# Plain projection weights: the low part starts as the negative of the high part, and a DMA adds the weights to it

## The chip, the cores and the metric

The kernel runs on one core of a Trainium2 chip. The metric is the device time of one execution in microseconds. The core has five engines that run side by side and wait for each other through semaphores: TensorE (PE in the profile, its weight loads PEld), VectorE (DVE), ScalarE (ACT), GpSimd (POOL) and SyncE (SP). SP, ACT and POOL can issue transfers (DMAs); 16 DMA engines carry them out. Each engine works through its own instructions in the order of the program.

## The reference

One decoder layer for 512 tokens of width 1024. What matters here is its first product, the input projection, which gives queries, keys and values of three attention groups, the input of a state space model, and gate logits:

```python
proj = x @ w_in[layer]
q = proj[..., :QKV_WIDTH]...
k = proj[..., QKV_WIDTH:2 * QKV_WIDTH]...
v = proj[..., 2 * QKV_WIDTH:3 * QKV_WIDTH]...
u = proj[..., 3 * QKV_WIDTH:3 * QKV_WIDTH + SSM_WIDTH]
gate_logits = proj[..., 3 * QKV_WIDTH + SSM_WIDTH:]
q = apply_rope(q, pos)
k = apply_rope(k, pos)
```

Behind it come windowed attention, the state space model `s5_ssm`, a merge with gates, an output projection, layer norm, a feed-forward network and a second layer norm. All of it is float32.

## The kernel before

**Products in three parts.** PE multiplies in a rounded float type (`F32R`). To keep float32's precision each operand is held as two tiles: `hi`, the value rounded to that type, and `lo`, the value less `hi`. `mm3` (lines 208 to 211) makes one product out of three matmuls: hi by hi, hi by lo, lo by hi. So every weight needs its `lo` before PE can get past the first matmul of a step.

**How weights arrive.** The class `Weights` (line 100) keeps a list of units. A unit is 128 x 2048 float32 (1 MB) in DRAM. SP loads it whole into a `raw` tile (`load`, lines 115 to 124; two such tiles). `split` (line 140) then turns one half of it, 128 x 1024, into a pair `whi`, `wlo`: ACT copies the half into `whi` (line 202), DVE subtracts `whi` from the raw half into `wlo` (line 203). There are three slots for such pairs. A step of the kernel uses one pair; at its end `release` frees the slot and calls `split` for the pair three steps ahead, whose ACT copy waits until PE has finished the step. After the second half of a unit `split` issues the next load.

**The steps.** The list `STEPS` has 36 entries, numbered n, one per weight pair: u (0 to 3), v of the first group (4 to 7), gates (8 to 19), k (20 to 23), q (24 to 27), v of the other two groups (28 to 35). Splits have the same numbers. Steps 0 to 3 have their own code, so the first split through the class is number 4; splits 4 to 35 belong to units of `w_in`. A step is 24 matmuls of 512 columns. Gate, k and q steps are `gate_tile` and `qk_tile` around `proj_tile`; v steps are `v_tiles`. Later stages (five "quads" of the input projection, then the GLU, branch, output and feed-forward weights) use the same class with other units, or write their own pairs.

**What else stands on the engines.** The order is written out by hand: `run_fill(n)` puts other work between or into the steps, by a table of step numbers (`at_step`). DVE carries the state space model's small operations, handed out a few at a time (`late`). ACT also copies x into time order (`copy_time`, line 510), copies u out (599), and applies the gates' function (958). POOL has little but DMAs. In step order these are: three parked gate blocks of 1 MB (`park_gates`, line 946); the rope's half turns, four adding DMAs of 32 partitions each after steps 21, 23, 25 and 27 (`turn_half`, line 768, called by `qk_tile` as soon as DVE has written its two rope products `kq` and `zk` or `zq`); and two loads of x in another order, 1 MB each (`fetch_x`, line 1068, at 30.6), which wait until the state space model's output has left the tile they go to (`ydr`).

Of the kernel before, what the change touches and what calls it, by code (L numbers as in the profile page):

```python
# [10 lines left out]
F32 = mybir.dt.float32  # L11
# [3 lines left out]
ALU = mybir.AluOpType  # L15
# [84 lines left out]
class Weights:  # L100


    def __init__(self, nc, pool, split):
        self.nc, self.split_to = nc, split
        self.units, self.raw, self.views = [], {}, {}
        self.free = deque((pool, n) for n in range(3))
        self.held = deque()
        self.pool = pool
        self.n_dma = self.n_split = 0
        self.jobs, self.loads, self.after, self.extra = {}, {}, None, None  # L110
# [29 lines left out]
    def split(self):  # L140
        n = self.n_split
        if n == 2 * len(self.units):
            return
        if self.jobs.get(n):
            self.jobs[n].popleft()()
            return
        self.flush()
        self.n_split += 1
        m, u = divmod(n, 2)
        slot = self.units[m][2]  # L150
        if slot is None:
            hi, lo = self.take_slot(n)
        else:
            z = slot(f"w{n}", F32R)
            hi, lo = z[:, 0:1024], z[:, 1024:2048]
        self.split_to(hi, lo, self.raw[m][:, 1024 * u : 1024 * (u + 1)])
        self.put(n, hi, lo)
        if u == 1:
            del self.raw[m]
            self.load()  # L160
# [14 lines left out]
def emit(ctx, tc, i, out):  # L175
# [42 lines left out]
    def kslice(pair, k, cols=slice(None)):  # L218
        return pair[0][k // 4][:, k % 4, cols], pair[1][k // 4][:, k % 4, cols]
# [21 lines left out]
    def home(n, name, dt=F32):  # L241
        return gat(n[1:], name, dt) if isinstance(n, str) else big(n, name, dt)

    w = Weights(nc, wp, split)
    out_homes = deque(("g0", 2, 6, 3))
    w.add(None, 8)
    for n in range(2, N_GLU, 2):
# [5 lines left out]
        else:  # L253
            w.add(i["w_in"][2 + 6 * g + 2 * "kqv".index(kind) + un], 2 if kind == "v" else 8)
    quad_first = 2 * len(w.units)
    for un in range(2):
        w.add(i["w_glu"][un], 4)
    for un in range(4):
# [235 lines left out]
    for k in range(KT):  # L494
        (xh, uh), (xl, ul) = ((z[k // 4][:, k % 4, :] for z in (xp[n], wup[n])) for n in range(2))
        raw = raws[k // 2][:, k % 2]
        if k == 0:
            late.take(4)
            continue
        for n, (hi, lo) in enumerate(((xh, xl), (uh, ul))):  # L500
            split(hi, lo, raw[:, 2 * n : 2 * n + 2].rearrange("p e c -> p (e c)"))
        late.take(4 if k < 2 else 10)
# [761 lines left out]
    for n in range(8):  # L1264
        ws = w.views[N_BR + n]
        src = (gh_, gl_) if n < 4 else (merged["h"], merged["l"])
# [21 lines left out]
        if n >= 4:  # L1288
            for ch, t0, _ in ts_:
                hi, lo = kslice(mx, ch)  # L1290
# [442 lines left out]
def build(inputs):  # L1733
    import concourse.bacc as bacc

    a = {k: np.asarray(v) for k, v in inputs.items()}
    arrays = {f"in_{k}": np.ascontiguousarray(v) for k, v in {**layout(a), **constants()}.items()}
    nc = bacc.Bacc("TRN2", target_bir_lowering=False, num_devices=1)
    aps = {k[3:]: nc.dram_tensor(k, v.shape, mybir.dt.from_np(v.dtype), kind="ExternalInput").ap()
           for k, v in arrays.items()}  # L1740
    out = nc.dram_tensor("out_dram", (S, D), F32, kind="ExternalOutput").ap()
    with tile.TileContext(nc) as tc:
        with ExitStack() as ctx:
            with tc.manual_schedule():
                emit(ctx, tc, aps, out)
    return nc, arrays
# [8 lines left out]
```

## Time and profile before

| | |
|---|---|
| time, median of 2 runs | 834.8 us (834.32 to 835.27) |
| the profiled execution | 835.37 us, span 833.6 us |
| granted TensorE clock, mean | 0.997 |
| PE busy | 822.0 us (99%) |
| DVE / ACT / POOL busy | 621.1 / 381.9 / 70.2 us |
| moved by DMA | 109.08 MB |
| queue 1 (SP), queue 0 (POOL), share of 16 engines | 31.9%, 8.8% |

The span runs from the first to the last instruction of the profiled execution; its own time has some more around it. Busy is the time in which an engine had an instruction in work. The strips of digits cut the span into 40 slices of 20.8 us; a digit is the busy share in tenths. A row of a timeline gives start, duration, engine, line, operation, tiles and in brackets the idle time before it with what ended that. A row of a table of stages gives the stretch, its length, busy time and number of instructions of each engine, the clock, the busy share of the DMA engines and GB/s. A queue's row gives packets, MB and the time its packets took as a share of 16 engines over the window asked for.

### The profile page before, as it was taken

The page shows a single profiled execution, that of the slowest core. Times are in us where ns is not written, and L with a number is a line of the kernel's source. Part 1 is how long each engine was busy: PE and PEld are TensorE (multiplying, and loading weights), DVE is VectorE, ACT ScalarE, POOL GpSimd, SP SyncE. Part 2 cuts the span into 40 slices and gives each one's busy share as a digit, 9 for nine tenths or more (in the row PEclk, how much of TensorE's full clock was granted, in tenths as well). Part 3 has the DMA queues.
Part 4 walks back from the last instruction along what each step waited for, and adds up shares of the span by engine and source line. Part 5 has one row for each costly group of instructions (what it writes and reads, how often), then busy time and mean ns, then how long its engine had stood idle before and what let it go on. Part 6 is the DMA issues. An engine that isn't in the chain of part 4 may idle for free.

```text
span 833.6 us, 13772 instructions
## 1 busy us (share of the span) xinstructions
PE 822.0 (99%) x5656; PEld 736.3 (88%) x5656; DVE 621.1 (75%) x1013; ACT 381.9 (46%) x579; POOL 70.2 (8%) x84
## 2 busy tenths in 40 slices
PE   9999999999999999999999999999999999999996
PEld 7888888888899989988888899999999999888885
DVE  6976899673879799556796798888888887523347
ACT  6964332145557535774242354445545456322210
POOL 0000001310011333000000410000000000000005
PEclk9999999999999999999999999999999999999998
DMA  8733534746235655651624162333322212722103
GB/s 336 190 106 137 161 138 127 167 117 198 77 88 141 129 107 112 210 208 51 252 101 152 51 223 87 112 118 114 107 101 101 103 52 101 303 101 87 65 1 101
DMA packets 29598, 109.08 MB, mean 131 GB/s; under 512 B 7392, under 2 KB 12256, under 8 KB 19936
## 3 DMA queue, kind: packets, MB, share of 16 engines
q1 hardware_dynamic: 23664, 90.79, 31.9%
q0 software_dynamic: 4240, 15.73, 8.8%
q10 hardware_dynamic: 1632, 1.70, 0.6%
q8 instruction: 44, 0.72, 0.4%
q14 instruction: 18, 0.15, 0.1%
HBM read 92.21 MB, written 9.70 MB: 122 GB/s over the span
## 4 chain that ended last, share of the span: by engine, by line
PE 68%; DVE 4%; DMA 2%; ACT 1%; issue 1%; POOL 0%; DVEq 0%; ACTq 0%
PE qx L1151 5%; PE dn L209 5%; PE dn L210 5%; PE dn L211 5%; PE qz L1151 2%; PE qy L1151 2%; PE wo L209 2%; PE wo L210 2%; PE b L210 2%; PE wo L211 2%; PE b L209 2%; PE b L211 2%; PE o L864 2%; PE fs9x L1498 1%; PE fs8x L1498 1%; PE fs7x L1498 1%
## 5 line engine op out<-in xcount | busy, mean ns | idle before, releaser
L203 DVE TENSOR_TENSOR wlo<-raw,whi 128x1024 fp32r<-128x1024 f32 x74 | 90.8, 1230 | 93.3 <-ACT whi L202 93.3
L202 ACT CAST whi<-raw 128x1024 fp32r<-128x1024 f32 x74 | 77.3, 1049 | 105.3 <-PE dn L211 63.5
L1466 ACT CAST whi<-sums 128x1024 fp32r<-128x1024 f32 x40 | 42.0, 1049 | 95.6 <-DVE sums L345 95.6
L209 PE MATMUL dn<-whi,ffh 128*128 128x512 f32 x168 | 65.4, 389 | 0.0
L210 PE MATMUL dn<-wlo,ffh 128*128 128x512 f32 x168 | 65.4, 389 | 0.0
L211 PE MATMUL dn<-whi,ffl 128*128 128x512 f32 x168 | 65.4, 389 | 0.0
L345 DVE TENSOR_TENSOR wlo<-sums,whi 128x1024 fp32r<-128x1024 f32 x40 | 48.7, 1220 | 0.0
L1122 ACT CAST whi_q<-rq 128x1024 fp32r<-128x1024 f32 x28 | 29.2, 1052 | 41.8 <-DVE rq L345 41.8
L345 DVE TENSOR_TENSOR wlo_q<-rq,whi_q 128x1024 fp32r<-128x1024 f32 x28 | 34.1, 1222 | 12.9 <-ACT whi_q L1122 12.6
L209 PE MATMUL pg<-x_hi,whi 128*128 128x512 f32 x96 | 37.6, 392 | 0.0
L210 PE MATMUL pg<-x_lo,whi 128*128 128x512 f32 x96 | 37.4, 389 | 0.0
L211 PEld LDWEIGHTS dn<-whi,ffl 128*128 128x128 f32 x168 | 31.5, 188 | 6.6
L211 PE MATMUL pg<-x_hi,wlo 128*128 128x512 f32 x96 | 37.4, 389 | 0.0
L209 PEld LDWEIGHTS dn<-whi,ffh 128*128 128x128 f32 x168 | 31.5, 188 | 6.6
L210 PEld LDWEIGHTS dn<-wlo,ffh 128*128 128x128 f32 x168 | 31.5, 188 | 6.4
L843 ACT ACTIVATE un<-un,st 128x256 f32<-128x256 f32 (+1 forms) x64 | 30.8, 483 | 13.2 <-DVE st L841 13.2
L768 POOL DMA_DIRECT2D kq<-qz x32 | 25.2, 1313 | 108.7 <-PE s L830 48.2
L1309 POOL TENSOR_TENSOR mvb<-mvb,epsb 128x1 f32<-128x1 f32 x4 | 3.9, 987 | 329.2 <-DVE mvb L337 329.2
L958 ACT ACTIVATE gt<-pg,bgate 128x512 f32<-128x512 f32 x12 | 8.3, 690 | 42.9 <-PE pg L211 42.9
L345 DVE TENSOR_TENSOR wlo<-ra,whi 128x1024 fp32r<-128x1024 f32 x20 | 24.4, 1222 | 1.8 <-ACT whi L1466 1.8
L209 PE MATMUL pv<-whi,x_hi 128*128 128x512 f32 x64 | 25.4, 396 | 0.0
L210 PE MATMUL pv<-wlo,x_hi 128*128 128x512 f32 x64 | 25.0, 390 | 0.0
(731 smaller groups left out, 2733.3 us busy)
## 6 DMA issues: line engine op xcount, KB each, us to landing
raw<-in_w_in SPq DMA_DIRECT2D x16, 1024.0 KB, 4.8
raw<-in_w_dn SPq DMA_DIRECT2D x11, 1024.0 KB, 4.8
ra<-in_w_gu SPq DMA_DIRECT2D x10, 1024.0 KB, 4.8
rb<-in_w_gu SPq DMA_DIRECT2D x10, 1024.0 KB, 4.8
rq<-in_w_quad SPq DMA_DIRECT2D x16, 512.0 KB, 4.3
kq<-qz POOLq DMA_DIRECT2D x32, 128.0 KB, 5.2
raw<-in_w_br SPq DMA_DIRECT2D x4, 1024.0 KB, 4.8
raw<-in_w_out SPq DMA_DIRECT2D x4, 1024.0 KB, 4.8
```

The lines of the kernel that those rows point to most:

```text
L202: act.copy(hi, src)
L203: dve.tensor_tensor(lo, src, hi.bitcast(F32), op=ALU.subtract)
L209: pe.matmul(dst, a[0], b[0], start=first, stop=False)
L210: pe.matmul(dst, a[0], b[1], start=False, stop=False)
L211: pe.matmul(dst, a[1], b[0], start=False, stop=last)
L345: eng.tensor_tensor(o, a, b, op=op)
L768: pool.dma_start(dst[32 * q : 32 * q + 32], z[32 * (q ^ 1) : 32 * (q ^ 1) + 32], accum_op=ALU.add)
L843: act.activation(pt, pt, AF.Exp, bias=mneg, scale=-1.0, accum_out=zsum)
L1122: act.copy(hi, src)
L1151: pe.matmul(d[:, 256 * e : 256 * e + 256], p_[:, e, k, :], q_[:, k, :], start=(first and e == k == m == 0), stop=(k == 3 and m == 2), skip ...
L1466: act.copy(hi, src)
L1498: pe.matmul(c, p_[:, e, k, :], q_[:, k, :], start=(b is not None and e == k == m == 0), stop=(k == 3 and m == 2), skip_group_check=True)
```

## The change

For the units of `w_in` (the first 18 units; `n_early` holds that number) `split` no longer lets DVE subtract. ACT copies the raw half into `whi` as before, ACT then writes minus `whi` into `wlo`, and POOL issues a DMA that reads the same half of the weights from DRAM a second time and adds it to `wlo`. All other weights are split as before. Splits 4 to 35 go this way, 32 in all.

```diff
         else:
             z = slot(f"w{n}", F32R)
             hi, lo = z[:, 0:1024], z[:, 1024:2048]
-        self.split_to(hi, lo, self.raw[m][:, 1024 * u : 1024 * (u + 1)])
+        src = self.raw[m][:, 1024 * u : 1024 * (u + 1)]
+        if m < self.n_early:
+            self.nc.scalar.copy(hi, src)
+            self.nc.scalar.mul(lo, hi.bitcast(F32), -1.0)
+            self.nc.gpsimd.dma_start(lo, self.units[m][0][:, 1024 * u : 1024 * (u + 1)], accum_op=ALU.add)
+        else:
+            self.split_to(hi, lo, src)
         self.put(n, hi, lo)
         if u == 1:
             del self.raw[m]
@@
     quad_first = 2 * len(w.units)
+    w.n_early = len(w.units)
     for un in range(2):
         w.add(i["w_glu"][un], 4)
```

On POOL, from the first parked gate block to the loads of x, the order before (`gdr` is the DRAM copy of a gate block, `kq` the tile that a rope turn adds to, `zk` and `zq` the products that it turns, `xf` x in another order):

```order
L946 DMA gdr<-gt_710 128x2048
L946 DMA gdr<-gt_986 128x2048
L946 DMA gdr<-gt_1166 128x2048
L768 DMA kq_1353<-zk_1352 32x2x512 x4
L768 DMA kq_1428<-zk_1427 32x2x512 x4
L768 DMA kq_1353<-zq_1498 32x2x512 x4
L768 DMA kq_1428<-zq_1567 32x2x512 x4
L1068 DMA xf_1909<-in_xk 128x2048
L1068 DMA xf_1911<-in_xk 128x2048
```

And now, from the first rope turn on (`wlo_24` is the low part for step 24; the lines are seven further on in the changed file):

```order
L775 DMA kq_1372<-zk_1371 32x2x512 x4
L160 DMA wlo_24_1417<-in_w_in 128x1024
L160 DMA wlo_25_1453<-in_w_in 128x1024
L775 DMA kq_1449<-zk_1448 32x2x512 x4
L160 DMA wlo_26_1492<-in_w_in 128x1024
L160 DMA wlo_27_1525<-in_w_in 128x1024
L775 DMA kq_1372<-zq_1521 32x2x512 x4
L160 DMA wlo_28_1563<-in_w_in 128x1024
```

The weights' DMA for split 24, 26 and 28 stands right behind the four DMAs of a rope turn. Further on in the same engine's order now, at the loads of x:

```order
L160 DMA wlo_32_1842<-in_w_in 128x1024
L160 DMA wlo_33_1919<-in_w_in 128x1024
L1075 DMA xf_1939<-in_xk 128x2048
L1075 DMA xf_1941<-in_xk 128x2048
L160 DMA wlo_34_1958<-in_w_in 128x1024
L160 DMA wlo_35_2015<-in_w_in 128x1024
```

Before, nothing stood behind the two loads of x until the next rope turn; now splits 34 and 35 do.

On ACT, at the first splits, the order before (`xt` is x in time order, `usb` the copy of u, `raw_128` the first unit):

```order
L510 COPY xt_262<-x_lo_95 128x2x4x128
L202 CAST whi_4_265<-raw_128 128x1024
L202 CAST whi_5_281<-raw_128 128x1024
L510 COPY xt_299<-x_hi_93 128x2x4x128
L510 COPY xt_299<-x_lo_95 128x2x4x128
L599 COPY usb<-pu_315 128x512
```

and now:

```order
L517 COPY xt_262<-x_lo_95 128x2x4x128
L158 CAST whi_4_265<-raw_128 128x1024
L159 ACTIVATE wlo_4_266<-whi_4_265 128x1024
L158 CAST whi_5_282<-raw_128 128x1024
L159 ACTIVATE wlo_5_283<-whi_5_282 128x1024
L517 COPY xt_301<-x_hi_93 128x2x4x128
L517 COPY xt_301<-x_lo_95 128x2x4x128
L606 COPY usb<-pu_317 128x512
```

Each copy has a negation behind it, and the copies of x and of u come after both.

## The prediction

> **What bounds the kernel now.** I read the page's busy row and its 40 slices first, then the waits of the tensor engine, then a table by stage, then timelines at the places where the change acts.
>
> ```profile
> PE 822.0 (99%) x5656; PEld 736.3 (88%) x5656; DVE 621.1 (75%) x1013; ACT 381.9 (46%) x579; POOL 70.2 (8%) x84
> PE   9999999999999999999999999999999999999996
> DMA  8733534746235655651624162333322212722103
> PE warm_b L289 <- DVE warm L285: 1.1, 1, 1.1
> PE fs10x L1498 <- DVE quad L345: 0.8, 1, 0.8
> PE qx L1151 <- ACT qsnap L1184: 0.7, 1, 0.7
> PE kb L566 <- issue: 0.5, 1, 0.5
> PE s L830 <- DMA kq<-qz: 0.4, 1, 0.4
> ```
>
> PE works without a gap: its five waits come to 3.5 us. So nothing taken off DVE can make the kernel faster by more than these, and only 0.5 us of them lies in the part that the change touches. What matters is whether the new way of making the second operand makes PE wait. The table by stage covers that part: 27 us (step 4, first use of such an operand) to 206 us (the last split, number 35).
>
> ```profile
> 27.00:60.00 33.00, 33.00 (x256) 27.39 (x259) 29.98 (x107) 24.72 (x28) 0.00 (x0) 1.00 0.61 160
> 60.00:126.00 66.00, 65.54 (x426) 54.29 (x419) 52.51 (x116) 24.02 (x31) 1.82 (x3) 1.00 0.42 143
> 126.00:180.00 54.00, 54.00 (x392) 44.83 (x394) 41.96 (x45) 14.21 (x21) 13.76 (x16) 1.00 0.60 132
> 180.00:206.00 26.00, 26.00 (x151) 21.22 (x143) 11.59 (x30) 14.66 (x33) 1.17 (x2) 1.00 0.61 199
> ```
>
> The columns are the stretch, its length, then busy us of PE, PE's weight loads, DVE, ACT and POOL, the clock, the DMA share and GB/s. PE is full in all four; ACT is fairly full in the first (24.72 of 33); DMA is busy 0.61, 0.42, 0.60 and 0.61, which is 20.1 + 27.7 + 32.4 + 15.9 = 96 us of 179.
>
> **What goes, what comes.** 32 splits change (numbers 4 to 35).
>
> ```profile
> L203 DVE TENSOR_TENSOR wlo<-raw,whi 128x1024 fp32r<-128x1024 f32 x74 | 90.8, 1230 | 93.3 <-ACT whi L202 93.3
> L202 ACT CAST whi<-raw 128x1024 fp32r<-128x1024 f32 x74 | 77.3, 1049 | 105.3 <-PE dn L211 63.5
> ```
>
> DVE loses 32 x 1.23 = 39 us. PE waited for DVE nowhere in this part, so that is worth nothing by itself. ACT gets 32 negations; none stands in the trace, and I price one as the copy of the same shape, 1.05 us: 34 us. POOL gets 32 issues and the DMA engines 32 transfers of 0.5 MB that add into their destination.
>
> *Price of one such transfer.* The only adding ones in the trace are the rope turns (kq, line 768; four of 128 KB make 0.5 MB), the nearest plain ones on the same queue are xf. The two rows are queue 0 from 138 to 149 us and from 197 to 206 us; packets, MB, share of 16 engines.
>
> ```profile
> q0 software_dynamic: 320, 0.52, 39.5%
> ...
> q0 software_dynamic: 288, 2.10, 57.4%
> ```
>
> The turns take 0.395 x 11 = 4.3 us per 0.5 MB. Plain: 0.574 x 9 = 5.2 us for 2.1 MB, 1.3 us per 0.5 MB. Adding needs two streams read (source, destination) where a plain transfer reads one, so 2.6 us is the low end, 4.3 the high one. I take 2.6: a turn reads and writes 32 partitions with both ends on chip, the new transfer has 128 partitions and one end in DRAM, as xf has. By the first price the load is 96 + 32 x 2.6 = 179 us for 179 us, by the second 234.
>
> *Latency in the gate steps (8 to 19).* Rows of ACT's timeline (start, us):
>
> ```profile
> 85.08 0.69 ACT L958 ACTIVATE gt<-pg,bgate 128x512 f32<-128x512 f32 x1 [3.81 <-PE pg L211]
> 90.52 0.69 ACT L958 ACTIVATE gt<-pg,bgate 128x512 f32<-128x512 f32 x1 [3.81 <-PE pg L211]
> 91.11 1.04 ACT L202 CAST whi<-raw 128x1024 fp32r<-128x1024 f32 x1
> ```
>
> A step lasts 5.44 us. Its slot is refilled for the step three later, so the refill has two steps, 10.9 us. From the step's end at 90.5: copy done 92.2, negation 93.2. From issue to the first bytes I read the DMA strip of 138 to 149 us (40 slices of 0.275 us) against POOL's row:
>
> ```profile
> 138.48 3.49 POOL L768 DMA_DIRECT2D kq<-zk  x4 [13.81 <-DMA raw<-in_w_in]
> DMA  5000000999937999979998872000199327999999
> ```
>
> Bytes flow from the eighth slice, 139.9: 1.45 us after the issue; they end near 145. So here bytes flow at 94.7 and end at 97.3, with a 0.2 us landing at 97.5; or at 100.1 where the 1 MB load of the next raw weights takes turns with them (2.6 us more). Due at 101.4. Covered by 1.3 to 3.9 us. Only the three parked gate blocks (1 MB each, 2.6 us ahead in the same queue) can break this: 0 to 3 us, I take 1. The Trainium skill, DMA: Bandwidth & Descriptors (Anatomy of one DMA), gives 2.0 us plus bytes over 436 GB/s for a transfer from this queue, an estimate of 3.2 us for 0.5 MB where my rows give 1.45 + 2.6 + 0.2 = 4.25; by it each refill would come 1 us sooner and the sum below fall by about 4. It names no price for adding.
>
> *Start (step 4).*
>
> ```profile
> 22.11 2.03 ACT L202 CAST whi<-raw 128x1024 fp32r<-128x1024 f32 x2
> 27.51 0.39 PE L210 MATMUL pv<-wlo,xt 128*128 128x512 f32 x1
> ```
>
> Copy 23.1, negation 24.1, bytes from 25.6 to 28.2, landed 28.4; PE wants it at 27.5. 0.9 us late, 3.5 beside a raw load. I take 1.5.
>
> *ACT up to 60 us.* It has 24.72 of 33 us; two negations push into it and six lie in it: 24.7 + 8.4 = 33.1. ACT is then full, and the copies of x in time order, of u and of the state inputs come up to 6 us later. PE has some of these one to two steps ahead. 0 to 6, I take 3.5.
>
> *The four rope turns (after steps 21, 23, 25, 27).* The new issue stands on POOL behind the turn's four issues, and those wait for DVE. Rows of ACT and DVE:
>
> ```profile
> 133.81 1.06 ACT L202 CAST whi<-raw 128x1024 fp32r<-128x1024 f32 x1 [4.38 <-PE pk L210]
> 137.09 1.08 DVE L345 TENSOR_TENSOR zk<-pk,rope 128x512 f32<-128x512 f32 x1
> 144.69 1.06 ACT L202 CAST whi<-raw 128x1024 fp32r<-128x1024 f32 x1 [4.38 <-PE pk L210]
> ```
>
> Step 21 ends at 133.8; zk is there 4.4 us later, the turn's bytes end at about 144.9, 11.1 us after the step, and the bytes for split 24 follow in the same queue: 11.1 + 2.6 + 0.2 = 13.9 us, due after 10.9. DVE is behind here because of queued state work and three subtractions; without the subtractions zk could come after its two products, about 2.2 us from the step's end, and all this 2.2 us sooner: 11.7, late by 0.8. With a raw load beside it 2.6 more, 3.4; with DVE as late as now, 5.6. Four times 0.8 to 5.6 is 3 to 22; I take 2.75 each, 11: half with a raw load, little DVE delay.
>
> *After 180 us.* The two xf loads wait on POOL for ydr and stand ahead of split 34.
>
> ```profile
> 197.28 1.17 POOL L1068 DMA_DIRECT2D xf<-in_xk  x2 [24.88 <-DMA ydr<-ysb]
> 203.48 1.05 ACT L202 CAST whi<-raw 128x1024 fp32r<-128x1024 f32 x1 [1.99 <-PE pv L211]
> ```
>
> Their 5.2 us of bytes end about 204, split 34's at 206.8; step 32 ends at 203.4 and step 34 starts one step after, about 208.9. Covered by 2 us; 0 to 3, I take 2, for the load of 0.61 + 3 x 2.6 / 26 = 0.91.
>
> Sum: 1 + 1.5 + 3.5 + 11 + 2 = 19 us, between 5 and 37 with all the ends. The profiled execution took 835.37 us (span 833.6), 0.6 above the median of 834.8: 835.4 + 19 = 854.
>
> **The rivals.**
>
> *A, the queue is full.* If an adding transfer costs what the turns show, 4.3 us, the load by stage (7, 12, 10 and 3 of the splits start in the four stretches, the first at 22 us) is 20.1 + 7 x 4.3 = 50 for 33, 27.7 + 12 x 4.3 = 79 for 66, 32.4 + 10 x 4.3 = 75 for 54, 15.9 + 3 x 4.3 = 29 for 26: 17 + 13 + 21 + 3 = 54 us over, and PE waits for all of it: 889. For it: it is the only adding transfer measured. Against it: the shape of the turns. The point of change is (179 - 96) / 32 = 2.6 us per transfer, so my own price sits on the edge.
>
> *B, not slower.* DVE is the place: with 39 us taken off it, zk comes 2.2 us after the step, the raw loads, which no longer wait for DVE's subtraction, fall before the turns, and each turn's bytes end early enough. Then split 24 lands within 10.9 us and only the start is late: 835 + 1.5, some 837. It decides at 0.8 us per turn, less than my reading of when the bytes end is worth. Against it: the stage from 126 to 180 us would have 32.4 + 26 = 58 us of DMA for 54.
>
> *C, the clock.* At the end of the kernel PE stops, and the clock goes:
>
> ```profile
> 825.41 0.28 PE L211 MATMUL dq<-whi,ffl 128*128 128x192 f32 x1
> 829.00:833.00 4.00, 0.00 (x0) 0.00 (x0) 0.61 (x1) 0.00 (x0) 0.00 (x0) 0.50 0.36 135
> ```
>
> It is halved about 3.3 us after the last matmul (the 0.50 begins a little before 829). Waits of that length in four to eight places would each be followed by work at half rate; if the clock comes back as slowly as it goes, 3.3 us at half rate lose 1.7 us each, 7 to 13 us more than the forecast, around 864. The Trainium skill, TensorE: Matmul & The Clock Gate (Part 1), says that an idle window of about 3.4 us halves the clock and that as much sustained work restores it; the end of this trace agrees with the first half, no row here shows the second.
>
> *D, faster.* A gain above 2% has no place: PE's waits are 3.5 us in all.
>
> **How the numbers follow.** Forecast 0.56, A 0.20, B 0.14, C 0.08, D or anything faster 0.02. The time is the forecast's, 854. Two per cent, about what a measurement of this kernel tells from no change, is 16.7 us, so the line is 851.5. The forecast's own range, 840 to 872, lies about two thirds above it: 0.38 slower, 0.18 within; with A and C slower is 0.66, with B same is 0.32. The range for 8 in 10 leaves most of B out below and the end of A above: 842 to 895.
>
> **What would show it.** Right: PE waits on `wlo` after steps 21 to 27 of 1 to 5 us each, waits at step 4 of 1 to 3 us, none above 1 us in the gate steps but after a parked block; ACT near 1.0 busy up to 60 us; queue 0 with about 2.6 us of engine time per new transfer; the clock at 1.00 throughout. Wrong: engine time near 4 us and PE waiting in every step from 8 on (A), no waits but the first (B), a clock under 1 between 27 and 240 us (C), or a negation or an issue on POOL that costs far more than the 1.05 and 0.9 us read here.

## The result, and the profile after

| | before | after |
|---|---|---|
| time, median | 834.8 us | 873.4 us (873.18 to 873.66) |
| ratio | | 1.0463, 95% between 1.0418 and 1.0508 |
| profiled execution, span | 833.6 us | 871.0 us |
| granted clock, mean | 0.997 | 0.981 |
| queue 0 (POOL's), MB and share of 16 engines | 15.73, 8.8% | 32.51, 18.9% |

The change costs 38.6 us. All times here are medians of fast executions; one execution of the kernel with 32 small DMAs took 1162.7 us at a granted clock of 0.654 and is not among them. The page of the kernel after, with the rows that answer to those of before: busy times, and the slices of PE, the clock and DMA.

```profile
PE 832.3 (96%) x5656; PEld 742.7 (85%) x5656; DVE 585.5 (67%) x981; ACT 416.0 (48%) x611; POOL 98.4 (11%) x116
PE   9799999779899999999999999999999999999995
PEclk9899999889989999999999999999999999999998
DMA  9986999894922655564254216223322322622103
```

DVE has lost 35.6 us of work and ACT has gained 34.1, nearly as the edit says, and neither matters. What matters is that PE, once at 9 in every slice but the last, shows three 7 and an 8 among its first eleven, that the clock's row shows an 8 in four places ahead of the last slice, and that DMA is at 8 or 9 in slices where it was at 3 to 7. The waits of PE in the kernel after (us in all, times, longest):

```profile
PE pv L216 <- DMA wlo<-in_w_in: 18.1, 3, 6.3
PE pq L217 <- DMA wlo<-in_w_in: 6.0, 1, 6.0
```

Four waits for the new transfer come to 24.1 us; nothing else on the list is above the 1.1 us that was the largest before. They lie at step 4, at splits 24 and 28, and at split 34. Each is followed by a stretch at half the clock. The chain that ended last, in order of time, shows the first (start, length, what):

```profile
24.15 9.38 DMA wlo<-in_w_in
...
33.57 0.80 PE pv L216
34.36 0.43 PE pv L217
...
39.41 0.24 PE pv L217
```

The transfer is issued at 24.15 and lands 9.4 us later. PE then goes on with one matmul per 0.43 us, and only from 39.4 with one per 0.23 us. The table by stage of the kernel after, the stages of before and one that takes in split 34, with the first stretch at half clock behind them (length, then busy us of PE, PE's weight loads, DVE, ACT, POOL, then clock, DMA share, GB/s):

```profile
27.00:60.00 33.00, 26.97 (x122) 21.75 (x124) 21.66 (x74) 24.11 (x26) 3.55 (x5) 0.90 1.01 239
60.00:126.00 66.00, 65.73 (x520) 54.46 (x513) 43.68 (x108) 38.89 (x45) 10.68 (x13) 1.00 0.83 202
126.00:180.00 54.00, 47.97 (x200) 38.96 (x199) 19.84 (x19) 19.38 (x20) 17.91 (x21) 0.94 0.91 208
180.00:245.00 65.00, 52.93 (x394) 42.61 (x394) 24.25 (x47) 32.38 (x57) 10.94 (x14) 0.91 0.80 190
32.40:39.20 6.80, 5.63 (x13) 4.46 (x14) 6.66 (x15) 5.58 (x4) 0.87 (x1) 0.50 1.07 284
```

The gate steps (60 to 126) are as full of PE as before although DMA went from 0.42 to 0.83. The two stages beside them miss 6.0 us of PE each, and there DMA is at 1.01 and 0.91. The last stage misses most, 12.1 us at an average of 0.80: it holds the waits of splits 28 and 34, and its average hides the full stretches in it. From 222 to 244 us, around split 34's transfer, the two queues hold

```profile
q0 software_dynamic: 717, 3.66, 66.5%
q1 hardware_dynamic: 720, 2.29, 29.3%
```

together 95.8% of the engines (queue 1 with two 1 MB loads of the quads' weights). In each of the four slow stretches PE works 5.3 to 5.9 us at 0.50; half of the 22.2 us that this makes, 11.1 us, is lost. What is left stands at the end of the kernel, POOL's last instruction, whose longest time is the third of the three numbers (ns), before and then after:

```profile
L1742 POOLq DRAIN  x3: 46/98/5772, 827.0 to 833.3; - x3
```

```profile
L1749 POOLq DRAIN  x3: 46/98/8387, 861.8 to 870.7; - x3
```

So the 37.4 us of longer span are 24.1 of waits, 11.1 of clock and 2.6 of a longer drain on POOL, with 0.4 left over the other way.

### The profile page after: what moved, and what is told of

It reads as the page before. It is cut to its first block, busy times and chain, and to the rows that moved or that the text cites. A ratio compares the mean times of both kernels' runs of the same rounds, so it can differ in the third digit from the quotient of the medians.

```text
span 871.0 us, 13824 instructions
## 1 busy us (share of the span) xinstructions
PE 832.3 (96%) x5656; PEld 742.7 (85%) x5656; DVE 585.5 (67%) x981; ACT 416.0 (48%) x611; POOL 98.4 (11%) x116
## 3 DMA queue, kind: packets, MB, share of 16 engines
q0 software_dynamic: 8848, 32.51, 18.9%
## 4 chain that ended last, share of the span: by engine, by line
PE 85%; DMA 7%; DVE 3%; ACT 2%; issue 1%; POOL 1%; ACTq 0%; DVEq 0%; SPq 0%
DMA wlo<-in_w_in 5%; PE qx L1158 5%; PE dn L217 4%; PE dn L215 4%; PE dn L216 4%; PE pv L216 3%; PE pg L215 3%; PE pv L217 3%; PE pg L217 3%; PE pg L216 2%; PE pv L215 2%; PE qz L1158 2%; PE qy L1158 2%; PE wo L215 2%; PE wo L216 2%; PE b L216 2%
## 5 line engine op out<-in xcount | busy, mean ns | idle before, releaser
L209 DVE TENSOR_TENSOR wlo<-raw,whi 128x1024 fp32r<-128x1024 f32 x42 | 51.7, 1235 | 70.6 <-ACT whi L208 70.6
L160 POOL DMA_DIRECT2D wlo<-in_w_in x32 | 33.3, 1041 | 162.9 <-ACT wlo L159 140.8
L352 DVE TENSOR_TENSOR wlo_q<-rq,whi_q 128x1024 fp32r<-128x1024 f32 x28 | 34.1, 1222 | 13.1 <-ACT whi_q L1129 13.0
L216 PE MATMUL pv<-wlo,x_hi 128*128 128x512 f32 x64 | 27.5, 429 | 12.1 <-DMA wlo<-in_w_in 12.1
L216 PE MATMUL pg<-x_lo,whi 128*128 128x512 f32 x96 | 37.4, 390 | 0.0
L217 PE MATMUL pg<-x_hi,wlo 128*128 128x512 f32 x96 | 37.4, 390 | 0.0
L217 PEld LDWEIGHTS dn<-whi,ffl 128*128 128x128 f32 x168 | 31.5, 188 | 6.6
L216 PEld LDWEIGHTS dn<-wlo,ffh 128*128 128x128 f32 x168 | 31.5, 188 | 6.6
L215 PEld LDWEIGHTS dn<-whi,ffh 128*128 128x128 f32 x168 | 31.5, 188 | 6.4
L159 ACT ACTIVATE wlo<-whi 128x1024 fp32r<-128x1024 f32 x32 | 33.9, 1061 | 1.0
```

The costliest lines, as they stand in the source:

```text
L159: self.nc.scalar.mul(lo, hi.bitcast(F32), -1.0)
L160: self.nc.gpsimd.dma_start(lo, self.units[m][0][:, 1024 * u : 1024 * (u + 1)], accum_op=ALU.add)
L209: dve.tensor_tensor(lo, src, hi.bitcast(F32), op=ALU.subtract)
L215: pe.matmul(dst, a[0], b[0], start=first, stop=False)
L216: pe.matmul(dst, a[0], b[1], start=False, stop=False)
L217: pe.matmul(dst, a[1], b[0], start=False, stop=last)
```

## The experiments

Two theories stood against each other at first. **Places and clock:** the four waits have each their own local cause (a queue order, a raw load), half-clock work follows each, and undoing the cause at the four places gives back nearly all. **Load:** the DMA engines have too much to do from 20 to 60 and 126 to 180 us, and a wait removed at one place turns up at the next. Where a kernel leaves out work, it is said.

### The four splits that wait, as before

```diff
-        if m < self.n_early:
+        if m < self.n_early and n not in (4, 24, 28, 34):
```

> Splits 4, 24, 28 and 34, the four for which PE waited in the trace of after, are made as before (DVE subtracts); the other 28 stay as in the change. Theory (four single places): the waits of 24.1 us and the 11.1 us at half clock behind them go, and four software DMAs fewer at the end: about 838 us. Rival (the DMA engines are full, so that any split can be the late one): the waits move to other splits, 26, 30 or 35 among them, and the time stays at 855 to 870 us.

Measured: 858.65 us, ratio 1.0273 (1.0247 to 1.0298). PE's waits in this kernel:

```profile
PE pq L217 <- DMA wlo<-in_w_in: 6.2, 2, 5.1
PE pv L216 <- DMA wlo<-in_w_in: 4.5, 3, 3.5
PE qx L1158 <- ACT v L809: 3.9, 1, 3.9
```

The four waits are gone, and new ones stand a little behind their places: at steps 6 and 7 (0.7 and 3.5 us), at splits 25 and 26 (1.0 and 5.1 us; they had none), and at the start of the first quad, 241 us, where ACT's copy of v is late. The clock falls three times. With four of 32 transfers away, 14.8 us of 38.6 came back, not the 35 of the first theory. The waits aren't owned by their splits.

### PE kept busy through the four waits

```diff
+    def keep_busy(b, a, z):
+        for _ in range(26):
+            pe.matmul(b, a, z, start=True, stop=True)
...
```

It is called ahead of steps 4, 24, 28 and 34 (the calls are left out here), with operands that are there already; what it writes is overwritten or never read.

> The changed kernel with 26 matmuls without use, 5.9 us, ahead of the first matmul of steps 4, 24, 28 and 34, so that PE works while it would wait. The data comes no sooner. Theory (the clock's fall is a cost of its own, 11.1 us): the four waits shrink to under 1 us each, the clock stays at 1.00, the time falls by 10 to 12 us to 861 to 863. Rival (the late transfers alone set the time, the slow stretch behind a wait is hidden by the next late transfer): 873, within 2 us.

Measured: 864.03 us, ratio 1.0351 (1.0336 to 1.0367). PE's timeline at step 4, and two stages of this kernel:

```profile
26.95 6.05 PE L596 MATMUL pv<-whi,x_hi 128*128 128x512 f32 x26
32.84 0.39 PE L215 MATMUL pv<-whi,xt 128*128 128x512 f32 x1
33.07 0.40 PE L216 MATMUL pv<-wlo,xt 128*128 128x512 f32 x1
```

```profile
27.00:60.00 33.00, 33.00 (x210) 27.44 (x209) 21.01 (x70) 26.62 (x30) 4.00 (x5) 1.00 1.02 244
126.00:180.00 54.00, 52.90 (x232) 43.12 (x231) 20.84 (x20) 17.88 (x19) 18.93 (x22) 1.00 0.94 207
```

PE does 6.05 us of idle work where it waited 6.03, and goes on at 0.23 us per matmul. The clock is 1.00 throughout, and the kernel is 9.4 us faster than with the same waits left empty. That is what the clock costs, 2.35 us per wait; the 11.1 us that the stretches add up to are 1.7 more, and this kernel has about as much in small waits of its own (span +28.3 = 24.2 of idle work + 2.6 of drain + 1.5). The Trainium skill, TensorE: Matmul & The Clock Gate (Part 1), has PE's clock halved by an idle window and restored by sustained work. These two kernels agree with both halves in kind: four falls, each in a wait of about 6 us, in the one and none in the other, and a clock of 1.00 again after 5.3 to 5.9 us of work.

### The adding transfer left out

```diff
-            self.nc.gpsimd.dma_start(lo, self.units[m][0][:, 1024 * u : 1024 * (u + 1)], accum_op=ALU.add)
```

The second operand stays minus the first, so the products are others; ACT's part of the change is all there.

> The adding DMA is left out for all 32 splits, so that the second operand stays minus the first: ACT's 32 negations and DVE's relief alone. Theory (the transfers do it all): no wait in this part, time as before the change, 834.8 within 1 us. Rival (ACT, full up to 60 us, delays what PE needs, the term that the prediction put at 3.5 us): 838 to 840, with waits of PE for ACT before 62 us.

Measured: 834.51 us, ratio 0.9997 (0.9987 to 1.0006). The first stage:

```profile
27.00:60.00 33.00, 33.00 (x265) 27.40 (x263) 21.61 (x72) 30.95 (x35) 0.00 (x0) 1.00 0.56 145
```

ACT is at 30.95 of 33 us and PE at 33.00 of 33. The whole cost hangs on the transfers; the negations together with DVE's relief come to 0.1 us, which is within noise.

### The same transfers without adding

```diff
-            self.nc.gpsimd.dma_start(lo, ..., accum_op=ALU.add)
+            self.nc.gpsimd.dma_start(lo, ...)
```

The transfer overwrites the negative, so again the products are others; bytes read, queue and order are those of the change.

> The same 32 transfers without adding, so that the second operand is overwritten by the weights (another product, the same bytes from DRAM, half the engine time per packet if reading the destination is what adding costs). Theory (a queue in order, shared with the raw loads, makes the four late): engine time per transfer 1.3 instead of 2.6 us, each of the four waits shorter by 1.3 to 3 us, those that stay above 3 us still with a fall of the clock: 850 to 863 us. Rival (adding is what makes them late): no wait above 1 us, about 838 us.

Measured: 858.01 us, ratio 1.0277 (1.0256 to 1.0297). Its waits, and its stages of the gate steps and of k and q:

```profile
PE pv L216 <- DMA wlo<-in_w_in: 9.0, 4, 5.0
PE pq L217 <- DMA wlo<-in_w_in: 4.7, 1, 4.7
```

```profile
60.00:126.00 66.00, 65.49 (x464) 54.25 (x463) 43.67 (x108) 36.70 (x43) 6.98 (x13) 1.00 0.65 212
126.00:180.00 54.00, 47.18 (x199) 38.25 (x197) 22.79 (x21) 19.61 (x19) 15.61 (x22) 0.94 0.77 213
```

Adding as such accounts for 15 of the 38.6 us. The other 23 come with 0.5 MB more in POOL's queue per split, whatever the transfer does. In the gate steps DMA is at 0.65, against 0.42 before and 0.83 after. Queue 0's packets of 4 KB there take 174 ns (median) where the adding ones take 328: 1.4 us for 0.5 MB, half the price, as expected. But splits 24 and 28 still wait 4.7 and 5.0 us in a stage whose DMA share is only 0.77: the turn, the transfer behind it and a raw load stand together there (142 to 154 us, from issue to landing of split 24, is at 0.95).

### The fifth unit's raw load one split later

After split 5 SP loads the next unit; with the subtractions gone it does so at 24.78 us, where before it was 26.79. This kernel holds that one load until split 6.

```diff
         if u == 1:
             del self.raw[m]
+        if u == 1 and m != 2 or n == 6:
             self.load()
```

> The changed kernel with the load of the fifth unit of raw weights issued behind split 6 instead of split 5, so that it no longer flows beside the transfer for split 4. Theory (the raw load, which in the change is issued 2 us earlier than before, takes turns with it): bytes from about 25.6 us, landed by 28.5, PE waits 1 us instead of 6.0 at step 4 and the clock does not fall there: 865 us. Rival (POOL's first DMA starts slowly by itself): bytes from 28 us all the same, wait of 3 to 4 us, about 870 us.

Measured: 877.04 us, ratio 1.0508 (1.0492 to 1.0523). What SP's queue moved from 25.4 to 26.4, and from 27.2 to 28.0 us, in the kernel after (packets, MB, share of the engines; no row for queue 0 in either):

```profile
q1 hardware_dynamic: 10, 0.08, 89.6%
...
q1 hardware_dynamic: 39, 0.32, 99.2%
```

In this kernel, what POOL's queue moved from 25.4 to 26.4 us, and the first use of the operand on PE's timeline:

```profile
q0 software_dynamic: 11, 0.05, 62.1%
```

```profile
29.59 0.50 PE L217 MATMUL pv<-wlo,xt 128*128 128x512 f32 x1 [2.24 <-DMA wlo<-in_w_in]
```

In the kernel after, SP's raw load, issued 0.6 us behind the adding transfer, has its first packets at 25.7 us and the engines to itself up to 28.0, with none of queue 0's packets among its own (the stretch between the two shown, 26.4 to 27.2, has 50.2%). With the load held back, the adding transfer flows from 25.7, 1.8 us after its issue, and the wait at step 4 falls from 6.0 to 2.2 us, without a fall of the clock. So the raw load owns 3.8 us of that wait, and the first bytes of POOL's first transfer are not slow by nature. But the load is then late itself, and so are those behind it. PE's waits in this kernel:

```profile
PE pv L217 <- DMA wlo<-in_w_in: 16.5, 4, 6.9
PE pq L218 <- DMA wlo<-in_w_in: 6.5, 1, 6.5
PE pg L218 <- DMA wlo<-in_w_in: 4.4, 2, 4.2
```

New waits at steps 7 and 8 (1.5 and 4.2 us) take more than step 4 gave, and those at splits 24, 28 and 34 are 0.1 to 0.6 us longer. The 865 us that the first theory expected were missed: the raw load that was held back makes PE wait later.

### The rope turns behind the splits

Each half turn is issued on POOL after the split that the end of its step allows, not ahead of it.

```diff
-            turn_half(dst, z)
+            turns.append((dst, z))
...
         w.release()
+        while turns:
+            turn_half(*turns.pop())
```

> The changed kernel with each rope turn issued on POOL behind the weights' transfer of the same step's end instead of ahead of it. Theory (splits 24 and 28 are late because they stand behind the turn): both waits, 12.3 us, and the 5.3 us at half clock behind them go: 856 us. Rival (the engines are full there, whatever the order): the waits stay or move to the next split, 870 us or more.

Measured: 858.1 us, ratio 1.0276 (1.026 to 1.0291), 2 us above the first theory's 856. Its waits and its stage of k and q steps:

```profile
PE pv L216 <- DMA wlo<-in_w_in: 11.9, 2, 6.1
PE pq L217 <- DMA wlo<-in_w_in: 2.5, 1, 2.5
```

```profile
126.00:180.00 54.00, 51.54 (x226) 41.68 (x225) 22.16 (x21) 21.77 (x22) 18.91 (x22) 1.00 1.01 231
```

The 12.3 us of waits at splits 24 and 28 are gone, with both falls of the clock; 2.5 us have come at split 25, which now is the first behind the turn. So the order on POOL is the cause of most of those two waits. DMA is at 1.01 in that stage; that what is left there is load is argued from this share alone.

### All three places at once

The late raw load, the turns behind the splits, and the loads of x behind split 34 (`at_step(31.5, fetch_x)` for 30.6).

> Late raw load, turns behind, and the two loads of x issued behind split 34: all 32 splits still by negation and adding transfer, only the order of queues changed. Theory: all four waits of about 6 us go with the clock's falls; what stays are a wait of 1 us at step 4 and 2.6 us of POOL's last DRAIN: 838 to 840 us. Rival (load): 850 us or more.

Measured: 861.98 us, ratio 1.032 (1.0303 to 1.0337). Its waits:

```profile
PE pv L217 <- DMA wlo<-in_w_in: 6.2, 3, 3.0
PE pg L218 <- DMA wlo<-in_w_in: 4.0, 2, 3.7
PE qx L1161 <- ACT v L812: 3.8, 1, 3.8
PE pq L218 <- DMA wlo<-in_w_in: 2.4, 1, 2.4
```

Not 838 to 840. With all three orders changed 16 us of waits remain, spread over seven places, so the theory that undoing the local causes gives back nearly all falls here. Nor does the kernel show load alone. The waits at steps 7 and 8 (0.7 and 3.7 us) come with the late raw load, as they did above (1.5 and 4.2), and the 3.0 us of the first line are at split 35, which now stands behind the loads of x. Each edit puts what it moved ahead of a later split. The clock falls five times, for 3.41 us each.

### Gate steps alone, and turns behind with splits 4 and 34 as before

```diff
-        if m < self.n_early:
+        if 8 <= n < 20:
```

> Only splits 8 to 19, the gate steps' weights, are made by negation and adding transfer; all others as before. Theory (a refill of 4 us of queue and bytes fits into two steps of 5.44 us where nothing else stands on POOL's queue but the parked gates): no wait of PE above 0.5 us, DRAIN longer by 12 x 82 ns: 835.8 us. Rival (the load, so that the raw loads and these transfers together make PE wait anywhere): 840 us or more.

Measured: 836.95 us, ratio 1.002 (1.001 to 1.0029), 1 us above the first theory. Its largest wait for a transfer and its stage of gate steps:

```profile
PE pg L217 <- DMA wlo<-in_w_in: 0.6, 1, 0.6
```

```profile
60.00:126.00 66.00, 65.14 (x412) 53.63 (x405) 41.25 (x106) 33.26 (x39) 9.50 (x12) 1.00 0.79 212
```

Twelve transfers at a DMA share of 0.79 cost 2 us, of which POOL's drain takes one (6.75 for 5.77 us). The other kernel is the one with the turns behind the splits, and:

```diff
-        if m < self.n_early:
+        if m < self.n_early and n not in (4, 34):
```

> Turns behind the weights' transfer, and splits 4 and 34 made as before: 30 of 32 splits stay changed. Theory (each remaining wait has its own place and they add up): of the 858.1 us with the turns behind, the waits of 11.9 us at steps 4 and 34 and the 5.6 us at half clock behind them go: 840 to 842 us. Rival (a wait that is removed lets the next transfers come late, as with the four splits made as before): 848 us or more.

Measured: 849.1 us, ratio 1.0164 (1.0144 to 1.0183): the side of the load theory. Its waits and two stages:

```profile
PE pv L216 <- DMA wlo<-in_w_in: 4.6, 2, 3.3
PE qx L1160 <- ACT v L811: 2.3, 1, 2.3
PE pq L217 <- DMA wlo<-in_w_in: 1.2, 1, 1.2
```

```profile
27.00:60.00 33.00, 28.41 (x186) 22.80 (x186) 23.15 (x90) 26.64 (x29) 4.20 (x5) 1.00 1.00 228
126.00:180.00 54.00, 52.80 (x316) 43.18 (x315) 23.48 (x23) 20.82 (x23) 22.90 (x27) 1.00 1.02 236
```

The first line is steps 6 and 7, the third split 25. DMA is at 1.00 and 1.02 where waits for transfers remain, against 0.79 in the gate steps above, where one of 0.6 us does. That the full engines make what is left of the waits is argued from this comparison and not shown; with the plain transfers PE waited in a stage at 0.77 too, behind the turns. That is the best of the versions that keep transfers outside the gate steps, and it is still 14 us behind the kernel before. None beats the kernel before.

### Small DMAs on POOL in the kernel before

The kernel before, with one small DMA (16 columns, to a tile that nothing reads) on POOL per split 4 to 35, and then with two:

```diff
         self.split_to(hi, lo, self.raw[m][:, 1024 * u : 1024 * (u + 1)])
+        if 4 <= n < 36:
+            z = self.pool.tile([P, 16], F32, tag="tiny", name=f"tiny{n}", bufs=4)
+            self.nc.gpsimd.dma_start(z, self.units[m][0][:, 0:16])
```

> The kernel before with 32 more DMAs on POOL, of 64 bytes for each partition into a tile that nobody reads, one at each of the same 32 splits. Theory (POOL's DRAIN at the end takes some 82 ns for each software DMA of the program: 5.77 us with 57, 8.39 with 89): DRAIN 8.4 us, time 834.8 + 2.6 = 837.4. Rival (the longer DRAIN comes from the bytes or from the adding): DRAIN 5.8 us, 834.8.

> The kernel before with two small DMAs on POOL, of 64 bytes for each partition, at each of the 32 splits: 64 more software DMAs than before. Theory (DRAIN is 82 ns for each): DRAIN 11.0 us, time 5.2 us above the kernel before, 840 us. Rival (the 3.2 us that 32 of them cost came from elsewhere, POOL's or the engines' work in the middle): DRAIN as with 32, 838 us, or PE waiting.

Measured: 838.11 us, ratio 1.0039 (1.0024 to 1.0053), and 841.6 us, ratio 1.0076 (1.0061 to 1.0091). POOL's drain with 64 small DMAs:

```profile
L1747 POOLq DRAIN  x3: 46/98/10998, 828.2 to 840.0; - x3
```

With 0, 12 (the gate steps above), 32 and 64 more DMAs on POOL the drain lasts 5.77, 6.75, 8.39 and 11.0 us: 82 ns for each DMA that POOL has issued in the program, small or large. It stands behind everything else, so all of it counts. The 32 cost 3.2 us where the drain explains 2.6, the 64 cost 6.7 where it explains 5.2, so both expected times were passed, by 0.7 and 1.6 us. With 64, PE's last matmul comes 1.15 us later than in the kernel before, and 0.75 of it is there by step 4. These small DMAs wait for nothing: the first is issued at 1.29 us, and at 8.87 PE waits 1.05 us for a weight of u from ACT, whose copies ahead of it wait 2.9 us for the load of x and these weights, where they waited 2.1 in the kernel before. So they seem to hold up the first loads; as this is one execution of each, that isn't shown.

## Why the prediction was right and wrong

**Right: nothing to gain.** That nothing taken off DVE can make the kernel faster by more than PE's few waits holds: with the transfers left out, the kernel is 0.1 us from the one before.

**Right: the prices.** A negation takes 1.06 us (1.05 was read from the copy). For the transfer, one stretch of 1.4 us in the gate steps of the kernel after, in which queue 0 moved nothing but one of them:

```profile
q0 software_dynamic: 71, 0.26, 94.5%
```

0.945 x 1.4 = 1.32 us for 0.26 MB, 2.6 us for 0.5: the low end, as taken. So rival A, which needs 4.3 us, isn't it, and the gate steps came out as rival A excludes: no wait in them, where 3.9 to 1.3 us of cover had been worked out (the 1 us for the parked blocks wasn't there either). The load of 179 us for 179 was read rightly, and too little was made of it. Put into rival A's table, 2.6 us gives 38 us of DMA for 33, 59 for 66, 58 for 54 and 24 for 26: two stages are too full, by 5 and 4 us, and steps 4, 24 and 28 lie in them.

**Wrong: the clock was made a rival of 0.08 and left out of the sum.** That is the largest step that failed: 9.4 us by the kept-busy kernel. The prediction's own upper ends, 3.5 us at step 4 and 5.6 at a turn, are longer than the 3.3 us at which it saw the clock go at the end of the kernel, so the forecast's case contained rival C's cause. Rival C's 7 to 13 us hold the 9.4, but partly by luck: it had 1.7 us at four to eight places, and 2.35 came at four. A clock under 1 between 27 and 240 us was named as its sign.

**Wrong in size: step 4.** 6.0 us for 1.5 (upper end 3.5). The raw load was expected to share the engines with the adding transfer; it was issued 2 us sooner than before, had the engines to itself from 25.7 to 28 us, and shared them after that. 3.8 of the 6.0 us are the raw load's. Some 2.2 us remain without it, more than the 0.9 worked out from copy, negation, latency and bytes. Most of the difference is in the bytes: in the kernel with the late raw load this transfer's packets run from 25.74 to 29.19 us, 3.45 us for the 2.6 of the sum, and it lands at 29.55 where 28.4 was worked out.

**Wrong in number and size: the turns.** 2.75 us at four places were forecast; 6.0 and 6.3 us at two came. That 12.3 is near the term's 11 is luck. POOL's timeline at the first one:

```profile
145.25 3.45 POOL L775 DMA_DIRECT2D kq<-zk  x4 [4.30 <-DVE zk L352]
147.45 2.21 POOL L160 DMA_DIRECT2D wlo<-in_w_in  x1
```

The mechanism is as described, and putting the turns behind the splits shows it (12.3 us gone, 2.5 new at the next split). DVE wasn't late either: zk is ready at 144.95, 2.3 us after ACT could start on the split, as the low end had it. But the transfer issued at 147.45 lands at 160.2, 12.7 us later, where the sum gave some 6 alone and 8 beside a raw load. From 148 to 162 the two queues hold

```profile
q0 software_dynamic: 697, 1.76, 73.8%
q1 hardware_dynamic: 144, 1.05, 24.9%
```

together 98.7% of the engines: the rest of the turn, the transfers of splits 24 and 25, and a raw load. The prediction added one raw load's half to the turn; it left out that the engines were behind already, with a parked gate block issued at 140.06 and split 23's transfer. The turns after steps 23 and 27 made no wait. The waits and slow stretches just before them, 6 us and about 3 us more, may be the time in which the queue caught up; the first experiment fits that, since with splits 24 and 28 taken out, split 26 waits 5.1 us.

**Wrong in size: split 34.** 5.8 us for 2, in the order that was shown: POOL issues the loads of x and then the weights. The upper end, 3, had no load of SP's in it, and the two 1 MB loads of the quads' weights shared the engines with this transfer (29.3% of them from 222 to 244 us).

**Wrong: ACT.** 3.5 us were put in for ACT being full up to 60 us. It is (30.95 of 33 with the transfers left out, forecast 33.1), and PE waits for none of it.

**Left out: the end.** The drain on POOL, 2.6 us, stood in the trace of before at 5.77 us, but not what it grows with.

In all: the sum's 19 us are 24.1 in waits, all at places that were named (two of the named ones, ACT and the parked blocks, made none), with 11.1 of work at half clock and 2.6 of drain that it didn't hold. Direction, places and the range of 842 to 895 held; the forecast's own 840 to 872 was passed by 1.4 us. Of the 19 us by which the value was low, some 5 are in the waits, where a transfer was priced as if it met engines with room in them, and the rest is the clock and the drain.

**Still open:** how much of the waits that are left with the orders changed is load, and the 1.15 us by which 64 small DMAs delay PE. The loads of x were moved only together with the two other places, so what split 34's wait owes to them alone wasn't tried.

## What to carry to other kernels

Where a change brings a stage's DMA share to 1.0 by its own price, price the waits from the load of the stage as well as place by place: here changing the order at one place moved a part of its wait to a split behind it, and only the gate steps, at 0.79 to 0.84, kept their transfers hidden. Take short stretches for it: 180 to 245 us averages 0.80, and the 22 us around split 34's transfer are at 0.96. On a kernel bound by PE, add to a wait the work at half clock that follows it, here about 2.4 us for each wait of 6 us. A DMA moved to POOL's queue has a price at the end of the program too, here 82 ns each.

## What the runs showed of the hardware that was not expected

- **POOL's drain at the end counts its DMAs.** 82 ns for each, from 57 (5.77 us) through 69 (6.75) and 89 (8.39) to 121 (11.0).
- **The slow clock comes in fixed lengths, on a fixed grid.** A fall ahead of the kernel's end lasts 3.41 or 6.83 us, and the falls of one trace begin whole multiples of 3.413 us apart (in the kernel after at 32.37, 158.67, 189.39 and 240.59 us: 37, 9 and 15 steps). So what a wait costs depends on where it lies. All 17 waits of 3.5 us or more in these kernels brought a fall, and four of the eight between 2.2 and 3.3 us: with the turns behind and splits 4 and 34 as before, one of 2.28 us did, inside one step of the grid, and one of 3.28 us, across two, didn't. Of the 21 falls, the 13 in which PE stayed away for 0.7 us or more after the start lasted 6.83 us, the other 8 lasted 3.41.
- **A later issue on SP's queue can overtake one on POOL's.** The raw load issued 0.6 us behind the adding transfer had its packets on the engines from 25.7 to 28.0 us (89.6%, 50.2% and 99.2% in three stretches) while the transfer had none.
- **An adding transfer takes nearly twice the engine time of a plain one**, 2.6 for 1.4 us per 0.5 MB (328 and 174 ns for a packet of 4 KB), at 128 partitions and from DRAM; the rope turns, 32 partitions and on chip, took 4.3.
